# LayerNorm's inverse square root: one square root on ScalarE and one reciprocal in place of ten VectorE instructions

## The chip, the core and the metric

One core of a Trainium2 chip runs the whole kernel. The metric is the device time of one execution in microseconds; lower is better. The kernel before was run three times and the median is taken. One further execution was recorded by the hardware profiler; every row below comes from that one.

## What is computed

A decoder trunk of two layers on one sequence of 512 tokens, model width 1024, all in float32. Each layer is a token mixer and a squared-ReLU MLP of width 4096, and after each of these four sub-layers the residual is added and a LayerNorm taken:

```python
def layer_norm(x, g, b):
    mu = jnp.mean(xf, axis=-1, keepdims=True)
    var = jnp.mean(jnp.square(xf - mu), axis=-1, keepdims=True)
    return (xf - mu) * lax.rsqrt(var + LN_EPS) * g + b

for layer in range(2):
    u = x * (1 + scale) + shift
    y = even_mixer(u) if layer == 0 else fox_attention(u)
    x = layer_norm(ALPHA * x + gate * y, ln_g[layer, 0], ln_b[layer, 0])
    u = x * (1 + scale) + shift
    y = square(relu(u @ w1 + b1)) @ w2 + b2
    x = layer_norm(ALPHA * x + gate * y, ln_g[layer, 1], ln_b[layer, 1])
```

Shift, scale and gate come from a conditioning vector. The even mixer is a gated recurrence beside a gated linear attention; the odd one is softmax attention with forget gates (16 heads of 64).

## The kernel before

The 512 tokens are four tiles of 128 tokens, `t` = 0 to 3; the model width is two halves of 512 columns, `h` = 0 and 1. The residual stream lies in eight tiles X[t][h] with the tokens on the partitions. Every float32 product is made of three matmuls: each operand is split into a rounded high part (a cast on ScalarE, `wh`, `uh`, `hh`) and a low part (a subtraction on VectorE or GpSimd, `wl`, `ul`, `hl`). Weights come in pieces of 1 MB (tiles `ws`) over the DMA queue of SyncE.

Four stretches take a LayerNorm. The first is at the end of `mix_out` (line 1004) after the even mixer; the second at the end of the first MLP (`after`, line 1179); the third in `mix_out` after the attention; the fourth in the last MLP, with a code of its own (`after`, line 1140). The first three call `normalize` (line 499) for each of the four tiles, twelve calls in all. `normalize` calls `stats` (line 488): two `bn_stats` and one `bn_aggr` give mean and variance (tile `mv`), epsilon is added (`ve`), and `rsqrt` (line 465) takes the inverse square root by an integer shift and three Newton steps: with `ve`, ten VectorE instructions on one column each (tiles `ve`, `rs_s`, `rs_i`, `rs_h`, `rs_t`, `rs_y`). Then two VectorE instructions write X[t][0] and X[t][1]. `rsqrt` is also called with 8 columns (line 944) and with 16 (line 1239).

After that, `to_u` (line 505) turns a tile round for the next product: TensorE transposes X[t][h] in pieces of 128 columns into a PSUM tile `pt`; the half h = 0 is scaled and shifted out of PSUM by four ScalarE instructions, the half h = 1 by four VectorE instructions (both write `u`); ScalarE casts `u` to `uh`, and GpSimd subtracts to get `ul`. The next product, `p` (an MLP) or `pqk` (the attention), reads `uh` and `ul`. In `mix_out` tile t − 2's `to_u` is written between the matmuls of tile t (tiles `pw`), and the MLP's first block (`up(0)`) starts on tiles 0 and 1 before tiles 2 and 3 are turned round. In the first MLP `mid` does the same in the last `down`.

The fourth stretch takes the inverse square root otherwise: a Sqrt on ScalarE with epsilon as its bias and a reciprocal on VectorE (lines 1152 and 1156), with `eps` set by GpSimd just before (line 1138).

Each engine runs its own instructions in order. Which order that is, is decided when the kernel is built: `TileContext(nc, schedule_with_timeline_sim=True)` lets a scheduler order the instructions of each engine by a simulated timeline; only where `order(...)` switches it on (the class `InOrder`, line 40, in the start of the kernel and a few short places) is the program's order kept. Since every instruction goes through the wrapper of that class, all rows name its line, L50; they are told apart by their tiles. A ScalarE function that the loaded table lacks needs an ACT_TABLE_LOAD first, which is put in when the kernel is built.

Of the kernel before, what the change touches and what calls it, by code (L numbers as in the profile page):

```python
# [8 lines left out]
F32 = mybir.dt.float32  # L9
# [3 lines left out]
AF = mybir.ActivationFunctionType  # L13
ALU = mybir.AluOpType
# [4 lines left out]
P = 128  # L19
# [6 lines left out]
LN_EPS = 1e-5  # L26
# [47 lines left out]
class Trunk:  # L74
# [26 lines left out]
    def setup(self):  # L101
        nc, i, c = self.nc, self.i, self.const
        self.ident = c.tile([P, P], F32, name="ident")
        make_identity(self.tc.nc, self.ident)
        self.ones = c.tile([P, P], F32, name="ones")
        nc.vector.memset(self.ones, 1.0)
        self.ones_r = c.tile([P, P], F32R, name="ones_r")
        nc.vector.tensor_copy(self.ones_r, self.ones)

        crow = c.tile([KC, P], F32, name="crow")  # L110
        nc.sync.dma_start(crow, i["c"].rearrange("o (k p) -> (o k) p", p=P))
        self.braw = self.s2("colB_raw")[:, :P]
        nc.scalar.dma_start(self.braw[:96], i["ada_b"].rearrange("l s (c p) -> (l s c) p", p=P))
        pc = self.ps()
        nc.tensor.transpose(pc[:, :KC], crow, self.ident[:KC, :KC])
        craw = c.tile([P, KC], F32, name="craw")
        nc.vector.tensor_copy(craw, pc[:, :KC])
        th = c.tile([P, KC], F32, name="cth")
        nc.scalar.activation(th, craw, AF.Tanh, scale=0.5)
        nc.vector.tensor_scalar(th, th, 0.5, 0.5, op0=ALU.mult, op1=ALU.add)  # L120
        self.cs = c.tile([P, KC], F32, name="cs")
        nc.vector.tensor_tensor(self.cs, th, craw, op=ALU.mult)

        self.shift, self.scale1 = {}, {}
        for n in range(4):
            self.shift[n] = c.tile([P, KC], F32, name=f"shift{n}")
            self.scale1[n] = c.tile([P, KC], F32, name=f"scale{n}")
        self.mod_d = {n: self.dram.tile([1, 2 * D], F32, name=f"modd{n}") for n in range(1, 4)}
        self.gate_d = {2: self.dram.tile([1, D], F32, name="gated2")}
# [179 lines left out]
    def plan_weights(self):  # L309
# [27 lines left out]
        n0 = len(L)  # L337
        out(i["ev_w_out"][0], 0)
        mlp(0)
        alternate(n0)  # L340
        win = i["od_w_in"][0]
# [5 lines left out]
        n0 = len(L)  # L347
        out(i["od_w_out"][0], 2)
        mlp(1)
        alternate(n0)  # L350
        self.wlist, self.n_dma, self.n_split, self.n_take = L, 0, 0, 0
# [113 lines left out]
    def rsqrt(self, v, n):  # L465
        nc = self.nc
        sh = self.tiny.tile([P, n], I32, tag=f"rs_s{n}", name="rs_s")
        nc.vector.tensor_scalar(sh, v.bitcast(I32), 1, None, op0=ALU.logical_shift_right)
        yi = self.tiny.tile([P, n], I32, tag=f"rs_i{n}", name="rs_i")

        nc.vector.tensor_scalar(yi, sh, -1.0, RSQRT_MAGIC - 2.0 ** 31, op0=ALU.mult, op1=ALU.add)
        hv = self.tiny.tile([P, n], F32, tag=f"rs_h{n}", name="rs_h")
        nc.vector.tensor_scalar(hv, v, 0.5, None, op0=ALU.mult)
        y = self.tiny.tile([P, n], F32, tag=f"rs_y{n}", name="rs_y")
        t = self.tiny.tile([P, n], F32, tag=f"rs_t{n}", name="rs_t")
        cur = yi.bitcast(F32)
        for _ in range(3):
            if n == 1:
                nc.vector.scalar_tensor_tensor(t, cur, hv, cur, op0=ALU.mult, op1=ALU.mult)
            else:  # L480
                nc.vector.tensor_tensor(t, cur, cur, op=ALU.mult)
                nc.vector.tensor_tensor(t, t, hv, op=ALU.mult)
            nc.vector.scalar_tensor_tensor(y, t, 1.5, cur, op0=ALU.subtract, op1=ALU.mult)
            cur = y
        return y


    def stats(self, z):
        nc = self.nc
        st = self.tiny.tile([P, 2, 6], F32, tag="st", name="st")  # L490
        for h in range(2):
            nc.vector.bn_stats(st[:, h], z[h])
        mv = self.tiny.tile([P, 2], F32, tag="mv", name="mv")
        nc.vector.bn_aggr(mv, st)
        ve = self.tiny.tile([P, 1], F32, tag="ve", name="ve")
        nc.vector.tensor_scalar(ve, mv[:, 1:2], LN_EPS, None, op0=ALU.add)
        return mv[:, 0:1], self.rsqrt(ve, 1)

    def normalize(self, z):
        nc = self.nc  # L500
# [542 lines left out]
    def mlp(self, l, X, rest, last):  # L1043
        nc, i = self.nc, self.i
        n = 2 * l + 1
        nb = 8

        def up(b):
            hh, hl = self.u8("hh"), self.u8("hl")
            ws = self.w_take() + self.w_take()  # L1050
            pts = [self.ps("p1") for _ in range(4)]
            if b == 0:

                part = lambda f, t0, t1: self.proj_late(pts[f][:, t0 * P:t1 * P], ws[f], t0 * P, t1 * P)
                part(0, 0, 2)
                rest(2)
                part(1, 0, 2)
                part(2, 0, 2)
                rest(3)
                part(3, 0, 2)  # L1060
            for f in range(4):
                if b == 0:
                    part(f, 2, 4)
                else:
                    self.proj_ch(pts[f], ws[f])
                if f % 2 == 0:
                    self.w_pre()
                col = 64 + l * 32 + b * 4 + f
                r, h2 = self.s2("r"), self.s2("h2")
                nc.scalar.activation(r, pts[f], AF.Relu, bias=self.colA[:, col:col + 1])  # L1070
                nc.scalar.activation(hh[:, f], r, AF.Square)
                nc.vector.tensor_tensor(h2, r, r, op=ALU.mult)
                nc.vector.tensor_tensor(hl[:, f], h2, hh[:, f].bitcast(F32), op=ALU.subtract)
                if b:
                    self.step(2)
                    if f % 2:
                        self.tick()
            return hh, hl

        def down(b, hh, hl, mid=None, after=None, byhalf=False):  # L1080
            ws = self.w_take() + self.w_take()
            for t in range(NT):
# [35 lines left out]
                if after is not None:  # L1118
                    after(t)
# [6 lines left out]
        for b in range(1, nb):  # L1126
            if b == 1 and last:
                self.ada = [self.ada_steps([(3, 4)], "g", True), self.ada_steps([(3, 5)], "v", True)]
            cur = up(b)
# [3 lines left out]
        if last:  # L1133
            g = self.bc(i["ln_g"][1, 1:2, :], "fg")
            bb = self.bc(i["ln_b"][1, 1:2, :], "fb")

            eps = self.const.tile([P, 1], F32, name="eps")
            nc.gpsimd.memset(eps, LN_EPS)

            def after(t):  # L1140
                end = t == NT - 1
                cols = [(h, c) for h in range(2) for c in (0, 256)] if end else [(0, None), (1, None)]
                part = lambda x, h, c: x[h] if c is None else x[h][:, c:c + 256]
                st = self.tiny.tile([P, len(cols), 6], F32, tag=f"st{len(cols)}", name="st")
                for q, (h, c) in enumerate(cols):
                    nc.vector.bn_stats(st[:, q], part(X[t], h, c))
                mv = self.tiny.tile([P, 2], F32, tag="mv", name="mv")
                nc.vector.bn_aggr(mv, st)
                mu = mv[:, 0:1]
                sd = self.tiny.tile([P, 3], F32, tag="sd", name="sd")  # L1150
                r = sd[:, 1:2]
                nc.scalar.activation(sd[:, 0:1], mv[:, 1:2], AF.Sqrt, bias=eps)
                onv = (0, 1) if end else (1,) if t == NT - 2 else ()
                for h in onv:
                    nc.vector.scalar_tensor_tensor(X[t][h], X[t][h], mu, g[h], op0=ALU.subtract, op1=ALU.mult)
                nc.vector.reciprocal(r, sd[:, 0:1])
                if not end:
                    nc.vector.tensor_scalar(sd[:, 2:3], mu, r, -1.0, op0=ALU.mult, op1=ALU.mult)
                for h, c in [(0, None)] + cols[2:] if end else cols:
                    x = part(X[t], h, c)  # L1160
                    if h in onv:
                        nc.vector.scalar_tensor_tensor(x, x, r, part(bb, h, c), op0=ALU.mult, op1=ALU.add)
                    else:
                        nc.scalar.activation(x, x, AF.Identity, scale=r, bias=sd[:, 2:3])
                        nc.gpsimd.tensor_tensor(x, x, g[h], op=ALU.mult)
                        nc.gpsimd.tensor_tensor(x, x, bb[h], op=ALU.add)
                    c0 = h * 512 + (c or 0)
                    nc.sync.dma_start(self.out[0, t * P:t * P + P, c0:c0 + x.shape[1]], x)

            down(nb - 1, *prev, after=after, byhalf=True)  # L1170
            return
        self.mod_load(n + 1)
# [372 lines left out]
```

## Time and profile before

| | |
|---|---|
| median of 3 runs | 1288.39 us (1285.93 to 1291.0) |
| profiled execution, its own time | 1284.24 us |
| its span, first to last instruction | 1282.5 us |
| mean granted clock of TensorE | 0.989 |
| ACT_TABLE_LOAD | 8, of 1.28 us |

In the rows, PE is TensorE's matmuls (PEld its weight loads), DVE VectorE, ACT ScalarE, POOL GpSimd. A row of a timeline has the start in us from the span's start, the time in us that the instruction, or a row of like ones, took (xN is their number), engine, line, operation, written tile <- read tiles, and the shapes. In square brackets stands how long the engine had been idle before and what released it. A row of waits has the engine and what it wrote, who released it, the total in us, the number of waits and the longest. In section 2 of the page the span is cut in 40 slices of 32 us; PEclk is the granted clock of TensorE in tenths.

### The profile page before, as it was taken

To read this page: it belongs to the slowest core of one execution; us is meant where nothing else is said; L and a number is where in the kernel's file an instruction comes from. 1 tells how busy PE (TensorE), PEld (TensorE's weight loads), DVE (VectorE), ACT (ScalarE), POOL (GpSimd) and SP (SyncE) were. 2 spreads that over 40 slices of the span, in tenths; PEclk is the share of its full clock that TensorE was granted. 3 is DMA by queue.
4 is the path that set the end of the run, shared out by engine and by line. 5 is a ranking of instruction groups with operands and counts; after the bars stand their busy time and mean duration, and the time that the engine had idled before them with its cause. 6 is when DMAs were issued, how large, how long until landed. Compare 5 with 4: busy or idle time off the path is not lost. (4 is left out here: it accounts for less than half of the span.)

```text
span 1282.5 us, 17949 instructions
## 1 busy us (share of the span) xinstructions
PE 1227.9 (96%) x6529; PEld 1043.9 (81%) x6529; DVE 935.4 (73%) x1578; ACT 583.2 (45%) x1014; POOL 514.7 (40%) x524
## 2 busy tenths in 40 slices
PE   5899899899999999999999999999799999999997
PEld 4687678798888888887999999887698888888886
DVE  7879888967878766879678878778967835443656
ACT  2375553353544443523566677752253433332321
POOL 3465421438312320375256557558429000000166
PEclk9899999999999999999999999999899999999999
DMA  9757425262775556523333132343253624132411
GB/s 280 212 198 261 166 67 164 83 218 79 246 246 182 181 197 230 178 85 101 99 97 87 53 92 79 108 164 99 83 175 121 198 82 131 66 107 91 132 33 66
DMA packets 131530, 177.52 MB, mean 138 GB/s; under 512 B 9270, under 2 KB 87764, under 8 KB 131442
## 3 DMA queue, kind: packets, MB, share of 16 engines
q1 hardware_dynamic: 131330, 176.33, 42.6%
q8 instruction: 51, 0.84, 0.3%
q14 instruction: 37, 0.30, 0.1%
q10 hardware_dynamic: 112, 0.05, 0.0%
HBM read 172.10 MB, written 4.26 MB: 138 GB/s over the span
## 5 line engine op out<-in xcount | busy, mean ns | idle before, releaser
L50 DVE TENSOR_TENSOR wl<-ws,wh 128x512 fp32r<-128x512 f32 (+1 forms) x255 | 270.8, 1087 | 66.9 <-ACT wh L50 62.2
L50 ACT CAST wh<-ws 128x1024 fp32r<-128x1024 f32 (+2 forms) x271 | 208.2, 810 | 200.9 <-PE p L50 80.9
L50 PE MATMUL p<-uh,wh 128*128 128x512 f32 (+1 forms) x576 | 207.1, 368 | 5.6 <-ACT uh L50 5.6
L50 PE MATMUL p<-uh,wl 128*128 128x512 f32 (+1 forms) x576 | 206.4, 366 | 0.0
L50 PE MATMUL p<-wh,hh 128*128 128x512 f32 (+1 forms) x516 | 201.0, 390 | 0.0
L50 PE MATMUL p<-wl,hh 128*128 128x512 f32 (+1 forms) x516 | 199.9, 387 | 0.0
L50 PE MATMUL p<-wh,hl 128*128 128x512 f32 (+1 forms) x516 | 199.9, 387 | 0.0
L50 PE MATMUL p<-ul,wh 128*128 128x512 f32 (+1 forms) x576 | 193.9, 368 | 0.5 <-POOL ul L50 0.5
L50 POOL TENSOR_TENSOR acc<-acc,ast 128x512 f32<-128x512 f32 x70 | 102.3, 1462 | 202.0 <-ACT ast L50 108.7
L50 DVE TENSOR_TENSOR h<-r 128x512 f32<-128x512 f32 x64 | 53.5, 839 | 121.8 <-ACT r L50 120.3
L50 PEld LDWEIGHTS p<-uh,wh 128*128 128x128 f32 x576 | 109.1, 189 | 24.1 <-ACT uh L50 6.7
L50 PEld LDWEIGHTS p<-uh,wl 128*128 128x128 f32 x576 | 109.2, 190 | 17.5
L50 PEld LDWEIGHTS p<-ul,wh 128*128 128x128 f32 x576 | 101.7, 191 | 18.1 <-POOL ul L50 0.7
L50 PEld LDWEIGHTS p<-wl,hh 128*128 128x128 f32 x516 | 96.9, 188 | 20.3 <-issue 0.5
L50 PEld LDWEIGHTS p<-wh,hh 128*128 128x128 f32 x516 | 96.9, 188 | 20.1 <-issue 0.5
L50 PEld LDWEIGHTS p<-wh,hl 128*128 128x128 f32 x516 | 96.9, 188 | 19.9
L50 POOL TENSOR_TENSOR ws<-ws,gate 128x512 f32<-128x512 f32 x16 | 25.0, 1598 | 211.3 <-DMA ws<-in_mlp_w_dram 211.3
L50 ACT ACTIVATE r<-p,colA 128x512 f32<-128x512 f32 x64 | 43.9, 686 | 143.4 <-PE p L50 143.0
L50 DVE SCALAR_TENSOR_TENSOR acc<-ast,cs,acc 128x512 f32<-128x512 f32 x70 | 83.7, 1195 | 15.2 <-DMA ast<-in_ada_w_dram 14.7
L50 DVE TENSOR_TENSOR Y<-Y,p 128x512 f32<-128x512 f32 x96 | 64.8, 682 | 41.0 <-PE p L50 40.3
L50 ACT ACTIVATE ast<-ast,cs 128x512 f32<-128x512 f32 x70 | 50.0, 723 | 95.7 <-DMA ast<-in_ada_w_dram 93.6
L50 POOL TENSOR_TENSOR ul<-u,uh 128x512 fp32r<-128x512 f32 x32 | 45.6, 1436 | 91.5 <-ACT uh L50 90.6
(322 smaller groups left out, 2699.8 us busy)
## 6 DMA issues: line engine op xcount, KB each, us to landing
ws<-in_mlp_w_dram SPq DMA_DIRECT2D x64, 1024.0 KB
ast<-in_ada_w_dram SPq DMA_DIRECT2D x160, 256.0 KB
ws<-in_od_w_in_dram SPq DMA_DIRECT2D x16, 1024.0 KB
ast<-in_ada_w_dram SPq DMA_DIRECT2D x16, 512.0 KB
ws<-in_ev_w_in_dram SPq DMA_DIRECT2D x7, 1024.0 KB
ws<-in_ev_w_out_dram SPq DMA_DIRECT2D x4, 1024.0 KB
nf<-fd SPq DMA_DIRECT2D x16, 256.0 KB
ws<-in_od_w_out_dram SPq DMA_DIRECT2D x4, 1024.0 KB
```

Of the source, the lines that this page charges most:

```text
L50: x = f(*a, **k)
```

## The change

`stats` no longer adds epsilon and calls `rsqrt`; it takes Sqrt of the variance with epsilon as bias on ScalarE and one reciprocal on VectorE. Twelve calls change. The epsilon tile is made in `setup` instead of in the last MLP, and the last MLP uses that one. `rsqrt` loses its form for one column; with 8 and 16 columns it does what it did.

```diff
@@ setup
+        self.eps = c.tile([P, 1], F32, name="eps")
+        nc.gpsimd.memset(self.eps, LN_EPS)
@@ rsqrt
         for _ in range(3):
-            if n == 1:
-                nc.vector.scalar_tensor_tensor(t, cur, hv, cur, op0=ALU.mult, op1=ALU.mult)
-            else:
-                nc.vector.tensor_tensor(t, cur, cur, op=ALU.mult)
-                nc.vector.tensor_tensor(t, t, hv, op=ALU.mult)
+            nc.vector.tensor_tensor(t, cur, cur, op=ALU.mult)
+            nc.vector.tensor_tensor(t, t, hv, op=ALU.mult)
             nc.vector.scalar_tensor_tensor(y, t, 1.5, cur, op0=ALU.subtract, op1=ALU.mult)
@@ stats
         nc.vector.bn_aggr(mv, st)
-        ve = self.tiny.tile([P, 1], F32, tag="ve", name="ve")
-        nc.vector.tensor_scalar(ve, mv[:, 1:2], LN_EPS, None, op0=ALU.add)
-        return mv[:, 0:1], self.rsqrt(ve, 1)
+        sd = self.tiny.tile([P, 2], F32, tag="sd2", name="sd")
+        nc.scalar.activation(sd[:, 0:1], mv[:, 1:2], AF.Sqrt, bias=self.eps)
+        nc.vector.reciprocal(sd[:, 1:2], sd[:, 0:1])
+        return mv[:, 0:1], sd[:, 1:2]
@@ mlp, the last one
-            eps = self.const.tile([P, 1], F32, name="eps")
-            nc.gpsimd.memset(eps, LN_EPS)
...
-                nc.scalar.activation(sd[:, 0:1], mv[:, 1:2], AF.Sqrt, bias=eps)
+                nc.scalar.activation(sd[:, 0:1], mv[:, 1:2], AF.Sqrt, bias=self.eps)
```

## Rows read from the trace of the kernel before

**Rows 1.** The page: busy time of each engine, and section 2's granted clock.

```profile
PE 1227.9 (96%) x6529; PEld 1043.9 (81%) x6529; DVE 935.4 (73%) x1578; ACT 583.2 (45%) x1014; POOL 514.7 (40%) x524
...
PEclk9899999999999999999999999999899999999999
```

**Rows 2.** The list of TensorE's waits over the whole span.

```profile
PE pt L50 <- DVE X L50: 7.5, 5, 3.0
```

**Rows 3.** Timeline of TensorE: matmuls with a wait, in the three stretches.

```profile
235.12 1.11 PE L50 MATMUL pt<-ident,X 128*128 128x128 f32 x8 [1.78 <-DVE X L50]
...
243.71 0.38 PE L50 MATMUL p<-uh,wh 128*128 128x256 f32 x1 [1.12 <-ACT uh L50]
...
246.84 0.74 PE L50 MATMUL p<-ul,wh 128*128 128x256 f32 x4 [0.48 <-POOL ul L50]
248.11 1.11 PE L50 MATMUL pt<-ident,X 128*128 128x128 f32 x8 [0.54 <-DVE X L50]
...
595.66 1.11 PE L50 MATMUL pt<-ident,X 128*128 128x128 f32 x8 [0.29 <-DVE X L50]
...
604.08 1.11 PE L50 MATMUL pt<-ident,X 128*128 128x128 f32 x8 [1.85 <-DVE X L50]
...
905.03 1.11 PE L50 MATMUL pt<-ident,X 128*128 128x128 f32 x8 [3.05 <-DVE X L50]
...
915.33 0.39 PE L50 MATMUL p<-uh,wh 128*128 128x256 f32 x1 [1.93 <-ACT uh L50]
...
919.15 0.58 PE L50 MATMUL p<-uh,wh 128*128 128x256 f32 x1 [2.61 <-ACT uh L50]
```

**Rows 4.** Windows: length; busy PE, PEld, DVE, ACT, POOL; PEclk, DMA share, GB/s.

```profile
915.00:920.00 5.00, 2.06 (x12) 1.86 (x13) 4.86 (x16) 0.90 (x2) 2.19 (x3) 0.76 0.00 0
920.00:925.00 5.00, 4.98 (x26) 4.68 (x26) 3.57 (x11) 1.71 (x5) 0.98 (x1) 0.56 0.02 5
925.00:930.00 5.00, 5.00 (x44) 5.00 (x43) 4.34 (x11) 1.04 (x2) 2.59 (x2) 1.00 0.00 0
```

**Rows 5.** Timeline of VectorE, third stretch: the chains of tiles 0, 1 and 2.

```profile
902.29 0.20 DVE L50 BATCH_NORM_AGGREGATE mv<-st 128x2 f32<-128x12 f32 x1
...
904.43 1.00 DVE L50 TENSOR_SCALAR X<-X,mv,rs_y 128x512 f32<-128x512 f32 x2
...
907.84 0.15 DVE L50 TENSOR_SCALAR ve<-mv 128x1 f32<-128x1 f32 x1
...
910.61 1.00 DVE L50 TENSOR_SCALAR X<-X,mv,rs_y 128x512 f32<-128x512 f32 x2
...
914.96 0.15 DVE L50 TENSOR_SCALAR ve<-mv 128x1 f32<-128x1 f32 x1
...
917.01 1.04 DVE L50 TENSOR_SCALAR u<-pt,G,B 128x128 f32<-128x128 f32 x3
...
919.76 1.24 DVE L50 SCALAR_TENSOR_TENSOR rs_y<-rs_t,rs_y 128x1 f32<-128x1 f32 x1
```

**Rows 6.** Timeline of all engines, fourth stretch: Sqrt and reciprocal of tile 0.

```profile
1259.21 0.21 DVE L50 BATCH_NORM_AGGREGATE mv<-st 128x2 f32<-128x12 f32 x1
1259.45 0.30 ACT L50 ACTIVATE sd<-mv,eps 128x1 f32<-128x1 f32 x1 [22.14 <-DVE mv L50]
1259.78 0.17 DVE L50 RECIPROCAL sd<-sd 128x1 f32<-128x1 f32 x1 [0.36 <-ACT sd L50]
```

**Rows 7.** Timeline of ScalarE: a table load, Sqrt (RB), Square (sq).

```profile
162.54 1.28 ACT L50 ACT_TABLE_LOAD   x1
163.84 1.68 ACT L50 ACTIVATE RB<-RB 128x512 f32<-128x512 f32 x3
...
166.21 0.37 ACT L50 ACTIVATE sq<-po 128x256 f32<-128x256 f32 x1
```

**Rows 8.** Timeline of ScalarE, third stretch: eviction of tile 0, casts.

```profile
905.73 1.51 ACT L50 ACTIVATE u<-pt,B,G 128x128 f32<-128x128 f32 x4 [8.07 <-PE pt L50]
...
918.48 0.62 ACT L50 CAST uh<-u 128x512 fp32r<-128x512 f32 x1 [3.20 <-DVE u L50]
```

## The prediction, made before the changed kernel was run

> **What bounds the kernel now.** The page comes first: TensorE is busy for 96% of the span, VectorE for 73%, ScalarE for 45% [rows 1]. So the kernel runs at TensorE's pace, and a cheaper VectorE or ScalarE instruction is worth only what TensorE stands still for it. The view to read next is therefore the list of TensorE's waits: transposes that wait for the normalized rows X come to 7.5 us in five waits [rows 2]. Reading that list stretch by stretch, between 260 and 590 us, between 640 and 870 us and after 925 us it has nothing above 1 us; what one of the three normalizing stretches gives to TensorE should thus reach the end undiminished. The timeline of TensorE shows each wait in these stretches [rows 3]:
>
> - first stretch (end of the first output projection, 228 to 262 us): 1.78 + 1.12 + 0.48 + 0.54 = 3.92 us;
> - second (end of the first MLP, 585 to 625 us): 0.29 + 1.85 = 2.14 us;
> - third (end of the second output projection, 885 to 945 us): 3.05 + 1.93 + 2.61 = 7.59 us.
>
> The third costs more than its waits. The granted clock there is 0.76 and then 0.56 of full speed after TensorE had stood still three times, and 1.00 in the next five microseconds [rows 4]; the lower level of 1.2 GHz held for part of these ten. From 920 to 925 us TensorE was busy for 4.98 us at 0.56, which is work for 2.8 us at full speed: 2.2 us lost. All waits and this loss together are 3.92 + 2.14 + 7.59 + 2.2 = 15.9 us, the most that a faster normalization can give.
>
> **The ten instructions, and what stands in their place.** Twelve tiles are normalized by the changed function, four in each stretch; the last four of the kernel have a square root on ScalarE already. In the third stretch tile 0 is the plainest case: its aggregate of mean and variance ends at 902.29 + 0.20 = 902.49 us and the first write to X begins at 904.43, so the ten instructions are 1.94 us in a row with nothing between them [rows 5]. The new pair has rows of its own in the last four tiles: aggregate until 1259.42, Sqrt 1259.45 to 1259.75, reciprocal 1259.78 to 1259.95 [rows 6], that is 0.53 us from aggregate to result, of which VectorE works 0.17. One tile alone gains 1.94 − 0.53 = 1.4 us. A tile whose chain runs between other work gains more, because each small instruction can be held up: one of them took 1.24 us [rows 5].
>
> **First stretch.** The wait of 1.78 us is for tile 0. Its chain gets at least 1.4 us shorter, more where other work had been put between, so I let it go whole. The 0.54 us wait for tile 2 goes too: two tiles before it have each given VectorE over 1 us. The 1.12 us is TensorE waiting for ScalarE's own eviction and cast, and the 0.48 us for GpSimd; nothing of the change touches them, and they are late next. Gain 2.3 us; ends 1.4 (tile 0 alone, at the plain 1.4) and 3.9.
>
> **Second stretch.** Both waits are for X, 0.29 and 1.85 us. By the second, two tiles' chains have become shorter. Gain 2.1 us; low end 1.4.
>
> **Third stretch.** Here VectorE's chain decides when TensorE's last wait ends: 919.15, released by a cast at 918.48 that itself waited 3.20 us for VectorE's u [rows 3, 8]. On that chain lie the ten of tile 0 (1.94 us), the ten of tile 1, from 907.84 to the write to X at 910.61, 2.77 us less about 0.35 for an eviction among them (three take 1.04), and what of tile 2 comes before the evictions, 914.96 to 917.01, 2.05 us [rows 5]. That is 6.4 us, replaced by three times 0.56 (0.53 and a hand-over), 1.7 us: 4.7 us. With the TensorE work that has to go in between I take 4.5. With waits of about 3 us instead of 7.6 I also expect the clock to stay up, as it did in the other two stretches, whose waits come to 3.9 and 2.1 us (of the 40 slices only the one at 32 us and the one at 898 us are under 0.9 [rows 1]); so 2.2 us more, 6.7 in all. Ends: 1.4 (tile 0 alone, and the clock falls again) and 9.8 (7.59 and 2.2).
>
> **What it adds.** The moved memset of epsilon costs nothing: it is one small instruction on GpSimd with no input, done long before the first Sqrt of a tile asks for it. The other callers of the old function, with 8 and 16 columns, keep their instructions.
>
> Table loads: Sqrt needs its table where Tanh or Exp ran before. I count one more in the first stretch, one in the third, and one before the forget gate's Exp, which now finds its table still there; the load ahead of the last four tiles goes, since nothing in between calls for another. A load takes 1.28 us: 162.54 to 163.82, and the next activation starts at 163.84 [rows 7]. In the stretches it hides in ScalarE's idle time, 8.07 us before the eviction at 905.73 [rows 8]; uncovered it would be 1.28 us each. At the forget gate TensorE is fed by other projections and shows no wait; with that cover gone, 1.28 us. A Square ran after Sqrt with no load between [rows 7], so the MLP's squares need none. No row shows a Relu there; if it is missing from that table, one load more in each of two MLPs, 2.6 us beside TensorE's long matmul streams. I take 0 for all of these; the upper end is the three, the two and a reload ahead of the second stretch, 6 × 1.28 = 7.7 us, all uncovered.
>
> The Trainium skill ("ScalarE: Activation LUTs", What ACT_TABLE_LOAD costs) puts a switch at about 2.66 us, a drain of 1.38 us after the load included, and under Table sets: the hidden batching unit asks that calls be batched by set, which speaks against this change. By that, three switches are an estimated 8.0 us of ScalarE time instead of 3.8. The trace does not agree: the next activation began 0.02 us after the load.
>
> The new wait is VectorE's reciprocal on ScalarE. Behind it on VectorE stand the two writes to X, the evictions of the tile before, and the next tile's sums; TensorE's transposes wait for all of these. Behind a waiting Sqrt on ScalarE stand evictions and casts, and behind those GpSimd's ul. With an idle ScalarE the price is in the 0.53 already. One reciprocal that is held up as the 1.24 us instruction was costs 1.1 us; I charge that once.
>
> **The sum.** 2.3 + 2.1 + 6.7 − 1.1 = 10.0 us. The profiled execution took 1284.24 us, so it would take 1274.2; it lies 4.1 us below the median of the runs, 1288.39, against which I forecast 1288.4 − 10.0 = **1278.4 us**.
>
> **The rivals.**
>
> *The wait moves instead of going.* The order of instructions on each engine is made anew when the kernel is built. If the transposes are put as much earlier among TensorE's matmuls as X comes earlier, the first wait of each stretch stays, and only the later ones and part of the clock go: say 0.54 + 1.0 + 2.5 = 4 us, 1284 us. For it: the transposes of the first and third stretch already stand before matmuls that need no X, and waited there. Against: the work left after the last wait is the same wherever the transposes stand.
> *ScalarE's queue holds VectorE up (slower).* If Sqrt stands behind the previous tile's eviction and casts, it waits up to 1.51 + 0.62 + 0.62 = 2.75 us [rows 8], and the reciprocal and all of VectorE with it: with 0.53 that is 3.3 us in place of 1.94, 1.3 us worse for each of the nine tiles that have one before them, 12 us; tile 0 of each stretch still gains, 4 us. Net 8 us: 1296 us. It decides from 1.4 us of foreign work ahead of Sqrt. For it: VectorE has hardly a pause in the third stretch, so each wait there is paid in full. Against: ScalarE was idle for 8.07 us before the first eviction there, and in the last four tiles Sqrt began 0.03 us after its aggregate.
>
> *The table loads lie open.* Each of the three added loads comes between an aggregate and its Sqrt, or ahead of work that TensorE waits for: 3 × 1.28 = 3.8 us of the 10.0 is given back, 1282.2 us, just inside what counts as no change. For it: Exp, Ln and Exp follow each other at the forget gate and leave a load no idle time. Against: the load before the last four tiles was over long before its Sqrt, which waited 22.14 us for its input [rows 6]. By the Trainium skill's batching rule and its 2.66 us for a switch (the page and sections named above) an estimated 8.0 us would go and 1286.4 us be left.
>
> *Nothing is gained.* The chain gets shorter but evictions and GpSimd's subtractions, late next, hold TensorE for as long: 1288 us. The 1.12 and 0.48 us waits speak for it, the nine writes and evictions that queue on VectorE against.
>
> **How the numbers follow.** A measurement of this kernel can tell about 0.5%, 6.4 us, from no change. The forecast (gain between 6.4 and 15.9) gets 0.60, the moved wait 0.16, the open table loads 0.05, nothing gained 0.10, ScalarE's queue 0.09. That makes faster 0.60, same 0.31, slower 0.09. The range reaches from the full 15.9 us, 1272.5, to no change, 1288.5; of the chances, it leaves out the slower case and a little at either end. Within the forecast alone it would be 1272.5 to 1282.
>
> **What would show it.** Right: the waits of 1.78, 0.54, 1.85 and 3.05 us are below 0.5 or gone, the third stretch's last wait ends 4 to 5 us earlier after its start, the clock there is 1.00, ten table loads stand in the profile, and the pair takes 0.5 to 0.6 us from aggregate to X. Wrong: Sqrt starts over 1.4 us after its aggregate in several tiles; TensorE waits for u or uh longer than before; a table load stands between an aggregate and its Sqrt; the clock still falls at 915 us; or waits appear in attention, where there are none now.

## The result, and the profile after

| | before | after |
|---|---|---|
| median of four runs each | 1287.16 us | 1273.14 us (1270.18 to 1276.4) |
| ratio of the runs, 95% interval | 1 | 0.9892 [0.9865, 0.9919] |
| second series, medians of 11 and 6 runs | 1286.78 us | 1273.88 us, 0.9902 [0.9882, 0.9922] |
| profiled execution, its span | 1282.5 us | 1274.7 us |

The changed kernel is 1.0 to 1.1% faster, 12.6 us by the second series of runs and 13.9 by the first; 10.0 were forecast. The profiled execution of the changed kernel took 1276.4 us, the longest of its four, so the two profiles stand only 7.8 us apart in span. What that gap is made of comes at the end of the experiments.

The page, section 1, which answers to [rows 1]:

```profile
PE 1226.4 (96%) x6529; PEld 1044.1 (82%) x6529; DVE 917.2 (72%) x1470; ACT 587.0 (46%) x1028; POOL 513.3 (40%) x524
```

Of the list of TensorE's waits, which answers to [rows 2], the lines that the text uses:

```profile
PE pt L50 <- DVE X L50: 4.8, 2, 3.3
...
PE pada L50 <- POOL acc L50: 2.5, 2, 1.3
...
PE pada L50 <- DVE acc L50: 0.7, 1, 0.7
```

VectorE has 108 instructions and 18.2 us of work less; TensorE's work is the same. The wait for X is down from 7.5 us in five waits to 4.8 us in two, and no wait of `p` for `uh` or `ul` is in the list any more. TensorE's timeline in the three stretches, all matmuls with a wait, which answers to [rows 3]:

```profile
234.82 1.11 PE L50 MATMUL pt<-ident,X 128*128 128x128 f32 x8 [1.48 <-DVE X L50]
...
898.05 1.97 PE L50 MATMUL pt<-ident,X 128*128 128x128 f32 x8 [3.35 <-DVE X L50]
```

Nine waits have become two: 3.92 us is 1.48 in the first stretch, 2.14 is nothing in the second, 7.59 is 3.35 in the third. The two that are left are the first of their stretch, and they are about as long as before (1.78 and 3.05). All others are gone.

Why the first ones stayed differs between the two stretches. In the third it is seen in the order: between the small product `pmod` and the first transposes TensorE did 44 matmuls `pw` before (891.67 to 901.99) and 36 after (886.20 to 894.70), at 0.23 us each 1.8 us fewer. The transposes were put that much earlier, and X, counted from `pmod`, came 1.5 us earlier.

In the first stretch the order is the same, 63 matmuls `pw` in both kernels. There the time from tile 0's aggregate to the first write to X fell by 2.56 us, from 3.81 to 1.25. But ahead of it stand the small VectorE instructions that fold scale and shift into the LayerNorm's weights (tiles `scale`, `G`, `B`), and one of these stood still in this execution while GpSimd subtracted. VectorE, and the subtraction of GpSimd beside it, first before and then after:

```profile
226.24 0.17 DVE L50 TENSOR_TENSOR B<-B,shift 128x8 f32<-128x8 f32 x1
226.33 2.40 POOL L50 TENSOR_TENSOR wl<-ws,wh 128x1024 fp32r<-128x1024 f32 x1 [0.23 <-ACT wh L50]
...
234.53 1.00 DVE L50 TENSOR_SCALAR X<-X,mv,rs_y 128x512 f32<-128x512 f32 x2
```

```profile
226.23 2.41 POOL L50 TENSOR_TENSOR wl<-ws,wh 128x1024 fp32r<-128x1024 f32 x1
226.25 2.41 DVE L50 TENSOR_TENSOR B<-B,shift 128x8 f32<-128x8 f32 x1
...
234.23 0.99 DVE L50 TENSOR_SCALAR X<-X,mv,sd 128x512 f32<-128x512 f32 x2
```

The hold took 2.24 us back, and X came only 0.30 us earlier. In the run with the later closing matmuls (last of the experiments but one), which has the same order in this stretch, the instruction was not held, and the first transposes do not wait (VectorE, TensorE):

```profile
225.13 0.17 DVE L50 TENSOR_TENSOR B<-B,shift 128x8 f32<-128x8 f32 x1
...
232.32 1.11 PE L50 MATMUL pt<-ident,X 128*128 128x128 f32 x8
```

The new pair in the third stretch, tile 0, VectorE's timeline (answers to [rows 5]) and then ScalarE's, with its table load:

```profile
896.69 0.19 DVE L50 BATCH_NORM_AGGREGATE mv<-st 128x2 f32<-128x12 f32 x1
...
897.25 0.16 DVE L50 RECIPROCAL sd<-sd 128x1 f32<-128x1 f32 x1 [0.28 <-ACT sd L50]
897.45 1.00 DVE L50 TENSOR_SCALAR X<-X,mv,sd 128x512 f32<-128x512 f32 x2
```

```profile
892.32 1.28 ACT L50 ACT_TABLE_LOAD   x1
896.92 0.29 ACT L50 ACTIVATE sd<-mv,eps 128x1 f32<-128x1 f32 x1 [3.32 <-DVE mv L50]
```

From the end of the aggregate (896.88) to the first write to X is 0.57 us, where it was 1.94. The load was over 3.3 us before Sqrt had its input. The granted clock of the third stretch, windows with the columns of [rows 4]:

```profile
895.00:900.00 5.00, 1.95 (x9) 1.95 (x10) 4.55 (x10) 0.29 (x1) 1.67 (x1) 0.67 0.67 198
900.00:905.00 5.00, 5.00 (x17) 3.92 (x16) 3.72 (x10) 2.93 (x7) 1.73 (x2) 0.65 0.57 208
905.00:910.00 5.00, 5.00 (x28) 4.21 (x27) 4.68 (x11) 2.83 (x7) 1.38 (x2) 1.00 0.00 0
```

It still falls for part of ten microseconds, only earlier in the stretch, behind the one wait that is left. And two waits are new. In the last MLP, TensorE's timeline:

```profile
1002.06 1.13 PE L50 MATMUL pada<-acc,ones 128*128 128x512 f32 x2 [1.18 <-POOL acc L50]
...
1003.88 1.12 PE L50 MATMUL pada<-acc,ones 128*128 128x512 f32 x2 [0.69 <-DVE acc L50]
```

In the kernel before TensorE has no wait after 925 us (its one wait of `pada`, 1.31 us, is at 111 us and is in both kernels). `pada` closes the sums of the last modulation, whose weights come by DMA. These DMAs are issued 8.0 us earlier than before (991.98, before 1000.01) and the sums end 7.8 us earlier, but TensorE gets there 10.0 us earlier, and 1.9 us of the gain are given back.

### The profile page after: what moved, and what is told of

Same layout as the page of the kernel before. It is cut to its first block, busy times and chain, and to the rows that moved or that the text cites. A ratio compares the mean times of both kernels' runs of the same rounds, so it can differ in the third digit from the quotient of the medians.

```text
span 1274.7 us, 17852 instructions
## 1 busy us (share of the span) xinstructions
PE 1226.4 (96%) x6529; PEld 1044.1 (82%) x6529; DVE 917.2 (72%) x1470; ACT 587.0 (46%) x1028; POOL 513.3 (40%) x524
```

## The experiments

Times are medians, ratios are to the kernel before on the same chip. Its median was 1287.22 us beside the first four kernels, 1286.78 beside the next four and 1285.84 beside the last four.

**One stretch at a time.** `normalize` gets a flag and takes the old or the new form:

```diff
-                    self.normalize(X[t])
+                    self.normalize(X[t], l == 1)
...
-            self.normalize(X[t])
+            self.normalize(X[t], False)
```

Third stretch alone:

> Sqrt and reciprocal in the third stretch alone; the first two keep the ten instructions. If each stretch gives what its own waits lose: TensorE's waits in the third fall from 7.6 to about 3.4 us, those of the first (3.9) and second (2.1) stay, and the time is 4 to 7 us below before (1280 to 1283), the granted clock deciding within that. If the gain comes from the order being made anew in the whole kernel, waits change in the first two stretches as well, and the time lies anywhere from before to after.

1280.65 us, 0.9955 [0.9937, 0.9972], 5.8 us. The third stretch has one wait left in the profile (3.27 us), the first two have all of theirs, with their transposes in the same places as before (the very first was 3.81 us long in this execution: the same fold instruction was held, 2.24 us for 0.17). As the first theory expected.

First and second alone (`l == 0`, `True`):

> Sqrt and reciprocal in the first and second stretch alone. If each stretch gives what its own waits lose: 3.9 falls to about 1.5 us, 2.1 to 0, the third stays at 7.6 with its fall of the clock, and the time is 4 to 5 us below before (1282 to 1283). If nearly all of the gain is the third stretch's and the clock's, it is within 2 us of before.

1277.38 us, 0.9933 [0.9914, 0.9953], 8.6 us, more than expected. The third stretch keeps its waits (2.86 + 0.89 + 2.17 + 0.60 = 6.5 us). Its profile shows why the recorded waits are too small a measure: from the start of the first wait to the last transposes of the first stretch it took 18.3 us where it was 21.5, 3.2 us less for 2.4 us of recorded waits and three waits fewer; the second stretch, from `pmod` to tile 2's transposes, took 29.6 for 32.2, 2.6 us less for 2.1 us and two waits fewer. A matmul is recorded as 0.39 us long while the next starts 0.23 us after it, so a wait that is counted from the end of one leaves 0.16 us out; here each interruption cost 0.2 to 0.25 more than its record. That makes 5.8 of the 8.6, just outside the interval (6.0 to 11.1), and in the same profile 1.7 us of waits for `pada` are given back in the last MLP. So 4 us or more of this one are open (the account comes back to it).

The parts, 5.8 and 8.6, add up to 14.4 us beside 12.6 and 13.9 for the whole, which is within their intervals. So each stretch gives its own share, and nothing can be seen that the new order gives elsewhere.

**Sqrt for nothing.** The table loads and ScalarE's part alone, with the ten instructions in their place:

```diff
         nc.vector.bn_aggr(mv, st)
+        sd = self.tiny.tile([P, 2], F32, tag="sd2", name="sd")
+        nc.scalar.activation(sd[:, 0:1], mv[:, 1:2], AF.Sqrt, bias=self.eps)
         ve = self.tiny.tile([P, 1], F32, tag="ve", name="ve")
```

> The ten instructions stay and give the result; Sqrt runs beside them on ScalarE and nothing reads it. It brings the table loads and ScalarE's part alone. If these lie hidden: within 2 us of before, ten or eleven table loads, none of them ahead of a wait of TensorE. If the loads lie open, 3.8 us slower (1291); by a price of 2.66 us for each switch, an estimated 8 us slower.

1287.32 us, 1.0012 [0.9995, 1.0029]. Ten loads, as in the changed kernel:

```profile
L50 ACT ACT_TABLE_LOAD x10 | 12.8, 1283 | 1.4 <-PEq L1531 1.2
```

Two more loads than before, and at most 3.7 us at the end of the interval, so three loads in the open (3.8) are just excluded and the loads lie hidden. The Trainium skill ("ScalarE: Activation LUTs", What ACT_TABLE_LOAD costs) would make it an estimated 8 us, three switches of 2.66; the rows have 1.28 us a load, and the time does not show even that.

**The ten for nothing.** Sqrt and reciprocal give the result, and the ten run beside them:

```diff
+        ve = self.tiny.tile([P, 1], F32, tag="ve", name="ve")
+        nc.vector.tensor_scalar(ve, mv[:, 1:2], LN_EPS, None, op0=ALU.add)
+        self.rsqrt(ve, 1)
         sd = self.tiny.tile([P, 2], F32, tag="sd2", name="sd")
         nc.scalar.activation(sd[:, 0:1], mv[:, 1:2], AF.Sqrt, bias=self.eps)
         nc.vector.reciprocal(sd[:, 1:2], sd[:, 0:1])
```

> Sqrt and reciprocal give the result; the ten instructions run as well, and nothing reads theirs. If VectorE's time is what counts (it has hardly a pause in the first and third stretch): most of the gain is lost there, waits of 6 us or more in the third, time 1 to 5 us below before (1282 to 1286). If the length of the chain from aggregate to X is what counts: waits as in the changed kernel, 3.4 us in the third, time 1272 to 1276.

1278.11 us, 0.9936 [0.9915, 0.9956], 8.2 us below before: between the two expectations. X no longer waits for the ten (VectorE's timeline, third stretch, tile 0):

```profile
896.21 0.19 DVE L50 BATCH_NORM_AGGREGATE mv<-st 128x2 f32<-128x12 f32 x1
...
896.77 0.16 DVE L50 RECIPROCAL sd<-sd 128x1 f32<-128x1 f32 x1
...
896.97 1.00 DVE L50 TENSOR_SCALAR X<-X,mv,sd 128x512 f32<-128x512 f32 x2
897.89 0.21 DVE L50 SCALAR_TENSOR_TENSOR rs_t<-rs_i,rs_h 128x1 f32<-128x1 f32 x1
```

but what stands behind them does. TensorE's waits in the third stretch:

```profile
897.57 1.11 PE L50 MATMUL pt<-ident,X 128*128 128x128 f32 x8 [3.34 <-DVE X L50]
...
910.31 0.39 PE L50 MATMUL p<-uh,wh 128*128 128x256 f32 x1 [0.94 <-ACT uh L50]
...
913.18 1.12 PE L50 MATMUL pt<-ident,X 128*128 128x128 f32 x4 [1.65 <-DVE X L50]
```

3.34 as in the changed kernel, then 0.94 and 1.65 that it does not have. So the shorter chain from aggregate to X is worth 8.2 us, the larger part (its interval reaches 2.6 us to either side), and the VectorE time that the ten gave back 12.6 − 8.2 = 4.4 us more, with some 3.7 us of uncertainty.

**The place of the transposes.** They are written behind all of a tile's matmuls:

```diff
-                self.mm3(pt, terms[:2], True, False)
+                self.mm3(pt, terms)
                 if h == 1 and t >= 2:
                     self.to_u(X[t - 2], t - 2, G, Bc)
-                self.mm3(pt, terms[2:], False, True)
```

> The changed kernel, with the transposes of tile t - 2 written behind all of tile t's matmuls instead of after the first six. If it is VectorE's chain that sets when the last wait of a stretch ends, wherever the transposes stand: the first waits shrink, waits for uh or ul appear instead, and the time is within 2 us of the changed kernel. If the place of the transposes is what costs: the first waits of 1.5 and 3.3 us go and nothing comes in their place, 4 to 6 us below the changed kernel.

1274.57 us, 0.9911 [0.9891, 0.9931], beside 0.9902 for the changed kernel. TensorE's waits in the third stretch:

```profile
896.76 1.12 PE L50 MATMUL pt<-ident,X 128*128 128x128 f32 x8 [0.21 <-DVE X L50]
...
907.23 0.39 PE L50 MATMUL p<-uh,wh 128*128 128x256 f32 x1 [2.99 <-ACT uh L50]
```

The first wait is gone and comes back further on. A wait of TensorE moves with the order; its sum in a stretch hardly changed (3.20 us here, 3.35 in the changed kernel).

**What leaves the first waits.** The changed kernel once more, as the measure for the next runs:

> The changed kernel once more, beside the next three on one chip, and for a second profile of it. 1270 to 1277 us; the first waits of the first and third stretch 1.5 and 3.3 us again, the transposes in the same places, ten table loads, waits of the ones matmul for acc in the last MLP again (1.9 us). Where the granted clock falls may differ from the first profile; its share of the time then shows in the difference of the two spans.

1273.88 us, with waits of 1.40 and 2.91 us. The clock fell in the same place, but at 0.66 for five microseconds and not for ten. The third stretch took 1.5 us less, half of what the spans (1274.7 and 1271.8) differ by: 0.4 in the first wait, and 1.1 from the first transposes to the last, where the clock is what differs. First the fold (`G, Bc = self.fold(n + 1)`) moved from the first tile of the second half to the last tile of the first half:

> The changed kernel, with the small VectorE instructions that fold scale and shift into the LayerNorm's weights (scale, G, B) moved ahead, to the last tile of the half before. If VectorE's work ahead of tile 0, stretched while GpSimd subtracts, is what leaves the first waits (1.5 and 3.3 us): both fall below 1 us, the clock stays up in the third stretch, 3 to 6 us below the changed kernel. If the transposes only move as much earlier again: the first waits stay above 1.2 and 2.5 us and the time is within 1.5 us of the changed kernel.

1272.84 us, 0.99 [0.9881, 0.9919]: no change beside 0.9902. But this did not do what it was meant to. The fold's small instructions came earlier in VectorE's order and still under GpSimd's subtractions, so the first wait of the third stretch was even longer, 4.91 us, and that of the first stretch gone. VectorE's timeline:

```profile
884.85 2.38 DVE L50 TENSOR_SCALAR scale<-scale 128x8 f32<-128x8 f32 x1
...
887.74 1.83 DVE L50 TENSOR_TENSOR G<-colA,scale 128x8 f32<-128x8 f32 x1
...
889.68 2.22 DVE L50 TENSOR_TENSOR B<-B,shift 128x8 f32<-128x8 f32 x1
```

Then GpSimd's subtractions (`wl`) given to VectorE, on top of the early fold and alone:

```diff
-                    self.w_pre(nc.gpsimd if h else None)
+                    self.w_pre()
```

> As the one with the early fold, and the weights' low parts of these stretches are subtracted by VectorE instead of GpSimd. It gives VectorE about 5 us more work in each of the first and third stretch and takes away GpSimd's hold on its small instructions. If that hold is the larger cost: 1 to 3 us below the one with the early fold. If VectorE's time is: first waits above 3 us, 2 to 6 us above it.

> The changed kernel with the weights' low parts of the first and third stretch on VectorE, and the fold where it was. If GpSimd's hold alone left the first waits of 1.4 and 2.9 us: as the run with both, 1265 to 1270, scale and G at 0.16 us instead of 2.4 and 1.8. If the earlier fold is needed too: 1270 to 1274, a first wait above 1 us left.

1267.05 us, 0.9855 [0.9833, 0.9876], with both, and 1268.07 us, 0.9859 [0.9839, 0.9878], with the subtractions alone: 5 to 6 us below the changed kernel, more than the 1 to 3 expected of the first, and the early fold is not needed. TensorE has no wait in the third stretch in either. The same instructions, alone:

```profile
891.63 0.17 DVE L50 TENSOR_SCALAR scale<-scale 128x8 f32<-128x8 f32 x1
...
892.31 0.15 DVE L50 TENSOR_TENSOR G<-colA,scale 128x8 f32<-128x8 f32 x1
...
892.57 0.17 DVE L50 TENSOR_TENSOR B<-B,shift 128x8 f32<-128x8 f32 x1
```

0.5 us in place of 6.4 in the run with the early fold. So GpSimd's hold on VectorE left the first waits.

**Is that hold also what made the ten dear?** The same edit on the kernel before:

> The kernel before, ten instructions and all, with the weights' low parts of the first and third stretch on VectorE. If GpSimd's hold on small instructions is most of what the ten cost: the same edit gives more here than on the changed kernel (over 7 us, to 1280 or less), and the change is worth under 9 us beside it. If the length of the chain is: it gives as much or less here (0 to 6 us, 1281 to 1287), and the change is worth 12 us or more beside it.

1279.93 us, 0.9956 [0.9939, 0.9974], 5.7 us, about what it gives on the changed kernel (0.9859 for 0.9902, 5.5 us). The gain is in the range that was expected if the length of the chain is what costs; the time is just below that range, 1279.93 for 1281 or more, with a median before that was lower on this chip. Beside it the change is worth 0.9956 − 0.9859, 12.5 us, as much as with the hold. Within some 4 us of uncertainty the two gains add up: the ten cost by the length of their chain and their number, and no cost of their being held can be seen.

**What was given back.** The closing matmuls of the last modulation come eight ticks later (a tick is one step of the sum, taken between the MLP's matmuls):

```diff
-        yield
+        for _ in range(8 if len(jobs) == 1 else 1):
+            yield
         if done:
             finish(*done)
```

> The changed kernel with the last modulation's closing matmuls (ones times acc) eight ticks later, so that their sums, which follow the loads, are there when TensorE comes to them. If these 1.9 us are given back by the change because TensorE now comes too early for the loads: the waits of pada in the last MLP go, 1 to 3 us below the changed kernel (1271 to 1273). If TensorE only meets another wait for the same loads, within 1 us of it.

1270.06 us, 0.988 [0.9859, 0.9901], by the medians 2.8 us below the changed kernel's 0.9902, and TensorE has no wait after 925 us. The waits went and none came in their place. That the time fell is not shown: the two intervals overlap, and in this profile the first stretch has no wait either, because the fold was not held there. With the early fold and the subtractions on VectorE as well:

> The fastest so far (early fold, low parts on VectorE) with the later closing matmuls. The wait of 0.6 us in the last MLP goes; 0.5 to 1.5 us below 1267, 1265 to 1267, if it gives what its wait shows, and no change if TensorE meets another wait.

1266.71 us, 0.9851 [0.9832, 0.987]: not to be told from 0.9855 without it. The fastest version is one of the three changed kernels with the subtractions on VectorE, about 1.5% below before and 0.4 to 0.5% below the changed kernel.

**The account.** By marks in the profiles the first stretch gave 3.2 us, the second 2.6; the third, from `pmod` to the last transposes, took 38.8 us before and 34.1 and 32.6 in the two profiles after, 4.7 and 6.2. Less 1.9 us of recorded waits, 2.3 with what each interruption costs beyond its record, given back in the last MLP, this makes 8.2 and 9.7 us. The spans differ from the one before by 7.8 and 10.7 us, so for the profiled executions the account closes to about 1 us.

The medians differ by more, 12.6 us, and what the executions without a profile did is not on record. Two things bear on it. The profile before has the fold instruction of the first stretch free, the two after have it held. From `pmod` to the last transposes this stretch took, with the ten, 36.3 us free and 39.6 held (before; the run with the third stretch alone, where the clock fell too), and with the pair 31.7 free and 33.1 held (the run with the later closing matmuls; after). Like with like it gives 4.6 or 6.6 us and not 3.2, which bears on the open part of the run with the first and second stretch alone as well. And the mean granted clock over a run was 0.9884 in the runs before and 0.9910 in those after (11 and 6 runs on one chip); 0.0026 of 1273 us is an estimated 3.3 us. A part of that lies within the stretches and is counted there already, so the two cannot be added, and how the rest divides is open.

## Why the prediction was right

The forecast lay 5.3 us above the measured time and its direction held. Step by step:

- **The mechanism held.** The gain came out of TensorE's waits in the three stretches, 13.65 us of them before and 4.83 after. The chain of the plain tile went from 1.94 to 0.57 us, as the sum had it (0.56). That the total came near is in part luck. By the first profile the stretches gave 1.6 us more than forecast, the clock's 2.2 and the 1.1 charged were not found, and 2.3 given back were not foreseen: 8.2 us for 10.0, with errors that go against each other.
- **First stretch**, 2.3 us forecast, 3.2 found. The step "I let it go whole" did not come out in either profile: the 1.78 us wait stayed at 1.48 and 1.40. The chain got 2.56 us shorter, enough for it, but the hold on a fold instruction ahead of it, for which the sum has no term, took 2.24 us back. Where the hold did not come, the wait went whole. The two waits that were to be "late next" (1.12 for ScalarE, 0.48 for GpSimd) went too: 15 matmuls `pw` stand between tile 1's transposes and `p` where 3 stood, 2.7 us more of work in which ScalarE and GpSimd can finish.
- **The rival of the moved wait** had the third stretch right: the transposes were put earlier by 1.8 us and the first wait stayed. In the first stretch the order did not change, and the wait stayed for another reason. It was wrong on what follows; the run with late transposes shows that the total does not hang on their place.
- **Second stretch**, 2.1 forecast, 2.6 found. Both waits went. The recorded wait leaves out the matmul's overlap, 0.2 to 0.25 us for each; this term was missing in all three stretches.
- **Third stretch**, 4.5 us without the clock, 4.7 and 6.2 found, of which 1.1 in the second is the clock's. The argument, by when the last wait ends, gave the right size, and it needed no guess about the order.
- **The clock** was the term in the wrong place: 2.2 us were to come back in the third stretch because the waits would be 3 us. They were, and it fell all the same in both profiles: in the first nothing of the 2.2 us came back, in the second about 1.1. Over whole runs the clock was higher after, an estimated 3.3 us, but not shown to be the third stretch's.
- **The held reciprocal**, 1.1 us charged: none was held. All sixteen took 0.148 to 0.165 us in the first profile. The hold fell on the fold beside it: in the second profile `B` took 2.19 us between tile 0's aggregate and X in the third stretch, and the chain was 2.22 us long there and not 0.57.
- **The table loads**: ten, where I had counted them (one in the first stretch, one in the third, one at the forget gate, the last one gone), and hidden, as the run with the unused Sqrt shows. No load stands in an MLP, so Relu and Square both run from Sqrt's table; the upper end of 7.7 us was too careful.
- **Given back**, 1.9 us: not foreseen. I read that TensorE had no wait in the last MLP and concluded that all of the gain would reach the end. A list of waits says what is late now, not what has little slack: the sums that TensorE found ready before were 1.2 us late for a TensorE that came 10.0 us earlier. In the run with the unused Sqrt, which gained nothing, the second of the two waits (0.69 us) stands already. In attention I took the waits for none; one of 0.83 us stood there (808.95, `pfg`), and it is 1.32 after.
- **ScalarE's queue**, the slower rival: Sqrt began 0.04 us after its aggregate in the plain tile; at worst a reciprocal waited 0.77 us (third tile, first stretch), and at worst Sqrt began 0.72 us after its aggregate, 0.87 in the second profile (third tile, third stretch). It never reached the 1.4 us from which it would have decided.

## What to carry to other kernels

A chain of ten one-column instructions costs by its latency, 1.94 us for ten, wherever an in-order engine waits for its end, and more by standing ahead of other work; a function on an idle engine and one hand-over each way took 0.57 us. To price such a change, ask when the last wait of the stretch ends and what sets that, and not which wait goes: the first waits here stayed and the sum went all the same. Then look for the loads that were just in time before: what runs ahead meets them. And compare two profiles of one kernel before explaining a wait: here one small instruction, held or not, decided whether the first stretch had its wait.

## What was not expected of the hardware

An 8-column VectorE instruction that takes 0.15 to 0.17 us took 1.8 to 2.4 us while GpSimd subtracted 1024 columns; with GpSimd idle, all three of the fold were plain. Some hundredths of a microsecond decided it in the first stretch: begun 0.09 us ahead of a subtraction, `B` took 0.17 us, begun 0.02 us behind one, 2.41. The Trainium skill ("SBUF — State Buffer", Who interferes with whom) says that GpSimd and those VectorE instructions that need the ports it shares with VectorE shut each other out: whichever issues first has them for its whole instruction, and the other fully blocks. This case agrees, and shows that giving VectorE the work itself was cheaper here, by 5 to 6 us.

The fall of the clock does not follow the length of the wait alone. Behind a first wait of 3.27 us in the third stretch, in the run with that stretch alone, the granted clock of the next ten microseconds stayed 1.00; behind 2.92 us in the run with the late closing matmuls it was 0.66 for five. What decides it was not tried.
